# One-hot matrices of a PEER expert mixer moved from GpSimd to VectorE, and adaLN columns fetched for two channel groups at once

## The chip, the cores and the metric

The kernel runs on one core of a Trainium2 chip. The metric is the device time of one execution in microseconds (us); less is better. The engines are TensorE (PE, with its weight loads PEld), VectorE (DVE), ScalarE (ACT), GpSimd (POOL) and SyncE (SP, which here only issues DMA transfers). Each engine runs its own instructions strictly in order and waits at an instruction until the semaphores that it needs have been raised.

## The reference

One decoder layer on a sequence of 1024 rows of 1024 channels. Cut to what matters here:

```python
mod = jnp.einsum('bd,de->be', silu_c, w_ada[l]) + b_ada[l]
shift1, scale1, gate1, shift2, scale2, gate2 = jnp.split(mod, 6, axis=-1)
h = modulate(rms_norm(x, norm1_w[l]), shift1, scale1)   # h * (1 + scale) + shift
proj = jnp.einsum('btd,de->bte', h, w_in[l])
...                                                     # GLA, gMLP, output projection
h2 = modulate(rms_norm(x, norm2_w[l]), shift2, scale2)
y2 = peer(h2, ...)     # for each row: 8 heads x 16 of 16384 experts
x = x + gate2[:, None, :] * y2

# in peer, for a block of 128 rows, ii its 128 expert numbers a row, gg their weights
u = expert_down[ii]
a = jax.nn.gelu(jnp.einsum('pd,ped->pe', xx, u), approximate=False)
vv = expert_up[ii]
return jnp.einsum('pe,ped->pd', gg * a, vv)
```

## The kernel before

**Start.** `x_first` loads the transposed input (8 tiles xt of 128x512, line L975), squares it and makes a row of reciprocal norms, `rrow`. `ada_cols(k)` makes the shift and scale columns (`mod`, `scol`) of channel group k (128 channels): it fetches 1 MB of w_ada in four transfers of 128x4x128 (`wada`, L902, runs of 512 bytes) and weights and sums its eight 128-row pieces into two accumulators `adc`, one for each half of w_ada's rows. The first piece of a half goes through ScalarE (L907), the other three through VectorE (L913, 128x256 each). TensorE then sums the accumulators over partitions (L918), and VectorE makes `mod` and `scol` (L919, L920). `h_first(k)` calls `ada_cols(k + 1)`, multiplies xt by `rrow` on GpSimd (L1004), and `h_split` makes the two halves hTh (ScalarE, L991) and hTl (VectorE, L996) of h, on which the matmuls of the first projection (mm, L173 to L175) wait. The weights of the projection, `wt`, come by the same queue of SyncE as `wada` (L1034) and are split into wh (ScalarE, L1037) and wl (GpSimd or VectorE, L1039).

**Middle.** From some 70 to 1390 us the dense projections, GLA, gMLP, routing, and from about 840 us the first blocks of the expert mixer, beside each other.

**Last stretch.** From 1390 us the remaining expert work runs alone, with its own pools (`own` is true). `peer_stream` walks a list of entries. A gather (GpSimd issues it, L442) brings for each of 128 lanes one row of 8 KB, an expert's u and v, into one of the buffers `uv`; VectorE forms the dot products with h (L496 twice an entry, or L452 once for a direct entry); ScalarE makes gelu and weight `r` and a weighted one-hot matrix `W` (L498 to L508; `rd`, `Wd` for a direct entry); TensorE adds W times v to `acc` (L515), which frees the buffer. Three small matrices steer this. `E` (L593, 128x256, from `ea` that ScalarE makes at L592 into its only buffer) selects which row of the block each lane serves. `e` (the tile `e2` of `entry_list`, L485, 128x128, one an entry, made 8 entries ahead) is the one-hot matrix that `W` is scaled from; its buffer is free once the `W` of nine entries before has been made. `Wr` (L533) is the same for rare rows. With `own`, all three are made on GpSimd, which also issues the gathers. The index of a gather comes from `ts_` (ScalarE, L467, two buffers) by `jk` (VectorE, L470 and L482).

Which engine makes what is written in the code; in what order an engine's instructions stand comes from a scheduler that simulates a timeline, so it can shift when a cost changes.

## Time and profile before

| quantity | value |
|---|---|
| median of 3 runs | 1671.41 us (1666.29 to 1672.44) |
| the profiled execution | 1661.6 us, span 1659.9 us |
| mean granted clock of TensorE | 0.936 |
| busy: PE, DVE, POOL, ACT | 1438.1, 1070.9, 887.5, 778.0 us |

The busy times are averages over stages: at the start (0 to 45 us) and in the holes of the last stretch TensorE is far from busy, and a change there is read from these windows, not from the share over the span. In a table of windows the busy columns stand in the order PE, PEld, DVE, ACT, POOL; a DMA share of about 1.0 means that all 16 DMA engines were moving data all the time.

### The profile page before, as it was taken

What the parts mean: (1) busy time and instruction counts of PE and PEld (TensorE: products, weight loads), DVE (VectorE), ACT (ScalarE), POOL (GpSimd) and SP (SyncE); (2) the same over time, 40 slices, a digit from 0 to 9 for tenths busy, and PEclk for the clock granted to TensorE, in tenths of its full rate; (3) what the DMA queues carried; (4) which work ended last, traced back from release to release, by engine and by line L of the source; (5) the groups of instructions that cost most, each with busy time, mean ns of one, the idle gap of its engine ahead of it and who ended that gap; (6) DMA issues with size and microseconds to landing.
All of it is one profiled execution on the core that took longest, in us unless ns stands there. A gap on an engine that the chain in (4) does not pass through costs nothing. (4 is left out here: it accounts for less than half of the span.)

```text
span 1659.9 us, 20529 instructions
## 1 busy us (share of the span) xinstructions
PE 1438.1 (87%) x6113; PEld 1078.2 (65%) x6113; DVE 1070.9 (65%) x2862; ACT 778.0 (47%) x1716; POOL 887.5 (53%) x761
## 2 busy tenths in 40 slices
PE   4999889999998998788889999989789954798894
PEld 2768757888768886567667777767578832353452
DVE  6773654111456469977987778788885476576653
ACT  4453323332446355735446665555455344444442
POOL 4232237543375338756666877556575425655750
PEclk7999989999999999999999999989899975899998
DMA  9643533223377338746756788768756364897992
GB/s 272 235 175 98 173 121 106 93 91 133 101 241 256 119 115 295 251 153 230 260 188 204 282 319 295 281 213 300 275 213 230 114 232 155 346 415 274 410 412 89
DMA packets 132635, 363.83 MB, mean 219 GB/s; under 512 B 17577, under 2 KB 36265, under 8 KB 116386
## 3 DMA queue, kind: packets, MB, share of 16 engines
q0 software_dynamic: 30816, 178.14, 28.5%
q1 hardware_dynamic: 78464, 132.15, 24.2%
q10 hardware_dynamic: 23234, 52.14, 8.8%
q8 instruction: 49, 0.80, 0.2%
q14 instruction: 72, 0.59, 0.1%
HBM read 336.44 MB, written 25.94 MB: 218 GB/s over the span
## 5 line engine op out<-in xcount | busy, mean ns | idle before, releaser
L1039 POOL TENSOR_TENSOR wl<-wt,wh 128x512 fp32r<-128x512 f32 x257 | 364.3, 1424 | 386.5 <-ACT wh L1037 328.1
L174 PE MATMUL mm<-wl,hTh 128*128 128x512 f32 x896 | 366.3, 409 | 10.3 <-DVE wl L1039 5.6
L1037 ACT ACTIVATE wh<-wt 128x512 fp32r<-128x512 f32 x368 | 228.4, 627 | 308.1 <-PE mm L175 184.8
L175 PE MATMUL mm<-wh,hTl 128*128 128x512 f32 x896 | 357.4, 404 | 3.0 <-DVE hTl L996 3.0
L173 PE MATMUL mm<-wh,hTh 128*128 128x512 f32 x896 | 339.5, 413 | 20.2 <-DVE sg L1240 6.4
L173 PEld LDWEIGHTS mm<-wh,hTh 128*128 128x128 f32 x896 | 172.8, 194 | 71.8 <-DVE sg L1240 7.7
L174 PEld LDWEIGHTS mm<-wl,hTh 128*128 128x128 f32 x896 | 173.2, 193 | 59.2 <-POOL wl L1039 9.2
L1039 DVE TENSOR_TENSOR wl<-wt,wh 128x512 fp32r<-128x512 f32 x111 | 100.0, 903 | 158.6 <-ACT wh L1037 146.4
L175 PEld LDWEIGHTS mm<-wh,hTl 128*128 128x128 f32 x896 | 172.6, 193 | 43.3 <-DVE hTl L996 3.1
L173 PE MATMUL mm<-hTh,wh 128*128 128x512 f32 (+1 forms) x448 | 167.2, 375 | 18.7 <-ACT hTh L169 6.4
L175 PE MATMUL mm<-hTh,wl 128*128 128x512 f32 (+1 forms) x448 | 158.2, 371 | 9.7 <-POOL wl L1039 7.2
L174 PE MATMUL mm<-hTl,wh 128*128 128x512 f32 (+1 forms) x448 | 163.9, 366 | 0.0
L442 POOL DMA_INDIRECT uv<-in_tab_dram,ix x94 | 102.7, 1093 | 71.6 <-PE acc L515 24.4
L496 DVE SCALAR_TENSOR_TENSOR uv<-uv,hps 128x512 f32<-128x512 f32 x148 | 97.8, 683 | 54.6 <-PE hps L495 33.3
L524 DVE SCALAR_TENSOR_TENSOR vl<-uv,r,vh 128x512 fp32r<-128x512 f32 x92 | 91.8, 1026 | 34.7 <-ACT vh L523 29.5
L173 PEld LDWEIGHTS mm<-hTh,wh 128*128 128x128 f32 x448 | 86.4, 194 | 35.4 <-ACT hTh L169 7.1
L515 PE MATMUL acc<-uv,W 128*128 128x512 f32 x192 | 98.9, 641 | 4.4 <-ACT W L508 2.9
L175 PEld LDWEIGHTS mm<-hTh,wl 128*128 128x128 f32 x448 | 85.6, 193 | 24.3 <-POOL wl L1039 8.2
L174 PEld LDWEIGHTS mm<-hTl,wh 128*128 128x128 f32 x448 | 86.5, 193 | 13.5 <-DVE hTl L170 0.2
L494 PE MATMUL hps<-hh,E 128*128 128x512 f32 x148 | 77.8, 529 | 17.7 <-DVE uv L496 12.3
L515 PE MATMUL acc<-uv,Wd 128*128 128x512 f32 x128 | 61.3, 628 | 9.1 <-ACT Wd L456 7.2
L186 DVE MAX8 tv<-so 128x8 f32<-128x128 f32 x128 | 28.5, 277 | 62.1 <-ACT so L1397 62.1
(955 smaller groups left out, 2727.9 us busy)
## 6 DMA issues: line engine op xcount, KB each, us to landing
wt<-in_w_inp_dram SPq DMA_DIRECT2D x224, 256.0 KB
wt<-in_w_qp_dram SPq DMA_DIRECT2D x80, 256.0 KB
wada<-in_w_ada_dram SPq DMA_DIRECT2D x32, 512.0 KB
wt<-in_w_outp_dram SPq DMA_DIRECT2D x64, 256.0 KB
wada<-in_w_ada_dram SPq DMA_DIRECT2D x32, 256.0 KB
s_d<-so ACTq DMA_DIRECT2D x32, 256.0 KB
xr<-in_x_dram ACTq DMA_DIRECT2D x8, 512.0 KB
x_d<-x ACTq DMA_DIRECT2D x8, 512.0 KB
```

The costliest lines, as they stand in the source:

```text
L173: nc.tensor.matmul(ps, lh, rh, start=first, stop=False)
L174: nc.tensor.matmul(ps, lh, rl, start=False, stop=False)
L175: return nc.tensor.matmul(ps, ll, rh, start=False, stop=last).ins
L186: nc.vector.max(v, st)
L442: nc.gpsimd.indirect_dma_start(out=uv[:], out_offset=None, in_=tab, in_offset=bass.IndirectOffsetOnAxis(ap=ix, axis=0))
L494: nc.tensor.matmul(hps, Ej, hh[:, sl], start=True, stop=False)
L496: nc.vector.scalar_tensor_tensor(uv[:, sl], uv[:, sl], 1.0, hps, op0=OP.mult, op1=OP.mult, accum_out=r[:, 2 + n:3 + n])
L515: nc.tensor.matmul(acc[:, sl], W, v[:, sl], start=first, stop=last)
L524: nc.vector.scalar_tensor_tensor(vl, v, r[:, 5:6], vh.bitcast(F32), op0=OP.mult, op1=OP.subtract)
L1037: nc.scalar.activation(wh, wt, AF.Identity)
L1039: eng.tensor_tensor(wl, wt, wh.bitcast(F32), op=OP.subtract)
```

## The change

Three edits. `E` is made on VectorE everywhere (the list `EP` goes). `e2` and `Wr` are made on VectorE when `own` is true. `ada_cols(kp)` serves two channel groups: its transfers are 128x2x256 (runs of 1 KB), still 32 transfers of 256 KB in all; an accumulator has 128x512 elements, so that ScalarE has 8 instructions in place of 16, VectorE 24 of 128x512 (L909) in place of 48 of 128x256, and `mod` and `scol` are made 4 times in place of 8. It is called for even k only.

```diff
--- before.py
+++ after.py
@@ -56,7 +56,6 @@
 RP2 = .42
 DA = 8
 FP = 15
-EP = (True,)
 WLM = 2
 WLM2 = 3
 WLM3 = 99
@@ -67,7 +66,6 @@
 VB = 2
 RA2 = 1.3
 RP3 = .5
-AS = 1
 HA = (range(8), ())
 YA = True
 YP = (4,)
@@ -482,7 +480,7 @@
         nc.vector.scalar_tensor_tensor(jk, ts_[:, 0:n], slot1[:, 0:1], ts_[:, 2 * n:3 * n],
                                        op0=OP.is_equal, op1=OP.mult, accum_out=r[:, 1:2])
         e2 = pq.tile([P, P], F32 if own else F32R, name="e2", bufs=pl["ahead"] + 2)
-        nc.gpsimd.tensor_scalar(e2, iota[:, int(lane0(b)):int(lane0(b)) + P], ts_[:, 3 * n:3 * n + 1], None, op0=OP.is_equal)
+        (nc.vector if own else nc.gpsimd).tensor_scalar(e2, iota[:, int(lane0(b)):int(lane0(b)) + P], ts_[:, 3 * n:3 * n + 1], None, op0=OP.is_equal)
         return pl, Ej, blk, r, uv, hr, e2
 
     def entry_dot(ent):
@@ -530,7 +528,7 @@
         y = ul.tile([P, 2 * D], F32, name="yr", tag="uv")
         nc.scalar.dma_start(y[:, :D], yr_d[gi])
         W = pl["pq"].tile([P, P], F32, name="Wr", tag="e2", bufs=pl["ahead"] + 2)
-        nc.gpsimd.tensor_scalar(W, iota[:, :P], rcol[gi][:, bi:bi + 1], None, op0=OP.is_equal)
+        (nc.vector if pl["own"] else nc.gpsimd).tensor_scalar(W, iota[:, :P], rcol[gi][:, bi:bi + 1], None, op0=OP.is_equal)
         return W, y
 
     def rare_keep(pl, gi, acc):
@@ -590,7 +588,7 @@
         ea = pl["pq"].tile([P, eb * P], F32, name="ea", bufs=1)
         E = pl["pq"].tile([P, eb * P], F32R, name="E", bufs=pl["ebufs"])
         nc.scalar.activation(ea[:, :n], iota[:, :n], AF.Abs, bias=mid[:, j:j + 1])
-        (nc.gpsimd if pl["own"] in EP else nc.vector).tensor_scalar(E[:, :n], ea[:, :n], hw[:, 1:2], None, op0=OP.is_le)
+        nc.vector.tensor_scalar(E[:, :n], ea[:, :n], hw[:, 1:2], None, op0=OP.is_le)
         return E
 
     def await_routing(b, done=routed):
@@ -893,31 +891,32 @@
                     nc.vector.scalar_tensor_tensor(acc, wt, sc[:, k:k + 1], acc, op0=OP.mult, op1=OP.add)
                 yield acc
 
-        def ada_cols(k):
+        def ada_cols(kp):
             accs = []
+            w2 = 2 * P
             for hf_ in range(2):
-                wa = t4("wada").rearrange("p (a c f) -> p a c f", a=4, c=2)
-                src = w_ada[hf_ * 512:(hf_ + 1) * 512, :].rearrange("(a p) n -> p a n", p=P)
-                for c in range(2):
-                    nc.sync.dma_start(wa[:, :, c], src[:, :, c * D + k * P:c * D + (k + 1) * P])
-                acc = gl.tile([P, 2, P], F32, name="adc", bufs=4)
+                acc = gl.tile([P, 2, w2], F32, name="adc", bufs=3)
                 for a in range(4):
-                    w_, s_ = wa[:, a], sc[:, 4 * hf_ + a:4 * hf_ + a + 1]
-                    if a < AS:
-                        nc.scalar.activation(acc if a == 0 else w_, w_, AF.Identity, scale=s_)
-                        if a:
-                            nc.gpsimd.tensor_tensor(acc, acc, w_, op=OP.add)
-                    elif a == 0:
-                        nc.vector.tensor_scalar(acc, w_, s_, None, op0=OP.mult)
+                    q = 4 * hf_ + a
+                    if a % 2 == 0:
+                        wa = t4("wada").rearrange("p (a c f) -> p a c f", a=2, c=2)
+                        src = w_ada[q * P:(q + 2) * P, :].rearrange("(a p) n -> p a n", p=P)
+                        for c in range(2):
+                            nc.sync.dma_start(wa[:, :, c], src[:, :, c * D + kp * w2:c * D + (kp + 1) * w2])
+                    if a == 0:
+                        nc.scalar.activation(acc, wa[:, 0], AF.Identity, scale=sc[:, q:q + 1])
                     else:
-                        nc.vector.scalar_tensor_tensor(acc, w_, s_, acc, op0=OP.mult, op1=OP.add)
+                        nc.vector.scalar_tensor_tensor(acc, wa[:, a % 2], sc[:, q:q + 1], acc, op0=OP.mult, op1=OP.add)
                 accs.append(acc)
-            ps = auxt([P, 2])
+            ps = auxt([P, 2, 2])
             for c in range(2):
-                for i, acc in enumerate(accs):
-                    nc.tensor.matmul(ps[:, c:c + 1], acc[:, c], ones[:, 0:1], start=i == 0, stop=i == 1)
-            nc.vector.tensor_tensor(mod[:, k:16:KD], ps, badat[:, k:16:KD], op=OP.add)
-            nc.vector.scalar_tensor_tensor(scol[:, k:k + 1], mod[:, KD + k:KD + k + 1], 1.0, n1t[:, k:k + 1],
+                for j in range(2):
+                    for i, acc in enumerate(accs):
+                        nc.tensor.matmul(ps[:, c, j:j + 1], acc[:, c, j * P:(j + 1) * P], ones[:, 0:1], start=i == 0, stop=i == 1)
+            ks = slice(2 * kp, 2 * kp + 2)
+            nc.vector.tensor_tensor(mod.rearrange("p (c k) -> p c k", c=2)[:, :, ks], ps,
+                                    badat.rearrange("p (c k) -> p c k", c=2)[:, :, ks], op=OP.add)
+            nc.vector.scalar_tensor_tensor(scol[:, ks], mod[:, KD + 2 * kp:KD + 2 * kp + 2], 1.0, n1t[:, ks],
                                            op0=OP.add, op1=OP.mult)
 
         def ada_row(c, r):
@@ -999,8 +998,8 @@
         ada_cols(0)
 
         def h_first(k):
-            if k + 1 < KD:
-                ada_cols(k + 1)
+            if k % 2 == 0 and k + 2 < KD:
+                ada_cols(k // 2 + 1)
             nc.gpsimd.tensor_tensor(xts[k], xts[k], rrow, op=OP.mult)
             h_split(k)
```

The lines of the changed kernel are numbered 2 lower up to L895 and 1 lower behind it. Where the scheduler puts the instructions, at three places:

VectorE at the start, before, from `dg` (a step of `rrow`) to the second hTl (`adc` are the accumulators, each row one or several instructions, xN their count):

```order
L944 TENSOR_TENSOR dg<-ident,rstd 128x512
L919 TENSOR_TENSOR mod<-aux,badat 128x2
L913 SCALAR_TENSOR_TENSOR adc<-wada,sc,adc 128x256
L920 SCALAR_TENSOR_TENSOR scol<-mod,n1t 128x1
L913 SCALAR_TENSOR_TENSOR adc<-wada,sc,adc 128x256 x4
L919 TENSOR_TENSOR mod<-aux,badat 128x2
L913 SCALAR_TENSOR_TENSOR adc<-wada,sc,adc 128x256
L920 SCALAR_TENSOR_TENSOR scol<-mod,n1t 128x1
L913 SCALAR_TENSOR_TENSOR adc<-wada,sc,adc 128x256 x4
L996 TENSOR_TENSOR hTl<-xt,hTh 128x512
L913 SCALAR_TENSOR_TENSOR adc<-wada,sc,adc 128x256 x2
L996 TENSOR_TENSOR hTl<-xt,hTh 128x512
```

VectorE at the same place, changed:

```order
L943 TENSOR_TENSOR dg<-ident,rstd 128x512
L909 SCALAR_TENSOR_TENSOR adc<-wada,sc,adc 128x512 x2
L1038 TENSOR_TENSOR wl<-wt,wh 128x512
L917 TENSOR_TENSOR mod<-aux,badat 128x2x2
L919 SCALAR_TENSOR_TENSOR scol<-mod,n1t 128x2
L909 SCALAR_TENSOR_TENSOR adc<-wada,sc,adc 128x512 x5
L995 TENSOR_TENSOR hTl<-xt,hTh 128x512 x2
L909 SCALAR_TENSOR_TENSOR adc<-wada,sc,adc 128x512
L917 TENSOR_TENSOR mod<-aux,badat 128x2x2
L919 SCALAR_TENSOR_TENSOR scol<-mod,n1t 128x2
```

Between the first `scol` and the first hTl nine instructions of 128x256, one `mod` and one `scol` stood; now five of 128x512 stand there, and the next `scol` comes for two groups at once.

GpSimd in the last stretch, before, some 1413 to 1440 us of the trace:

```order
L442 DMA uv<-in_tab_dram,dix_147 128x2048
L485 TENSOR_SCALAR e_12855<-iota,ts__12845 128x128
L593 TENSOR_SCALAR E<-ea,hw 128x256
L485 TENSOR_SCALAR e_12903<-iota,ts__12893 128x128
L485 TENSOR_SCALAR e_12925<-iota,ts__12915 128x128
L593 TENSOR_SCALAR E<-ea,hw 128x256
L485 TENSOR_SCALAR e_12959<-iota,ts__12949 128x128
L485 TENSOR_SCALAR e_12988<-iota,ts__12978 128x128
L593 TENSOR_SCALAR E<-ea,hw 128x256
L485 TENSOR_SCALAR e_13026<-iota,ts__13016 128x128
L275 TENSOR_TENSOR tl<-tsel,th 128x112
L442 DMA uv<-in_tab_dram,ix 128x2048 x2
L442 DMA uv<-in_tab_dram,dix_147 128x2048
L442 DMA uv<-in_tab_dram,ix 128x2048 x6
```

GpSimd at the same place, changed (`tl` is a step of the routing):

```order
L440 DMA uv<-in_tab_dram,dix_147 128x2048
L273 TENSOR_TENSOR tl<-tsel,th 128x112
L440 DMA uv<-in_tab_dram,dix_147 128x2048 x2
L273 TENSOR_TENSOR tl<-tsel,th 128x112
L440 DMA uv<-in_tab_dram,ix 128x2048 x2
L440 DMA uv<-in_tab_dram,dix_147 128x2048
L440 DMA uv<-in_tab_dram,ix 128x2048 x11
```

The six `e` and three `E` that stood between two gathers have left; two `tl` are all that stands among the gathers now.

VectorE in the last stretch, before, some 1507 to 1530 us of the trace:

```order
L432 TENSOR_TENSOR hl<-h2l,hh 128x1024
L165 TENSOR_SCALAR fs<-fs 128x1
L496 SCALAR_TENSOR_TENSOR uv,r<-uv,hps 128x512 x2
L573 SCALAR_TENSOR_TENSOR fin<-fin,fs,fw 128x1024
L452 SCALAR_TENSOR_TENSOR uv,rd<-uv,h2l 128x1024 x2
L564 TENSOR_TENSOR fin<-acc,g2row 128x1024
L452 SCALAR_TENSOR_TENSOR uv,rd<-uv,h2l 128x1024 x5
L565 TENSOR_TENSOR fin<-fin 128x1024
L470 SCALAR_TENSOR_TENSOR jk,r<-ts__13709,slot_65 128x16
L470 SCALAR_TENSOR_TENSOR jk,r<-ts__13731,slot_65 128x16
```

VectorE at the same place, changed:

```order
L591 TENSOR_SCALAR E<-ea,hw 128x256
L571 SCALAR_TENSOR_TENSOR fin<-fin,fs,fw 128x1024
L494 SCALAR_TENSOR_TENSOR uv,r<-uv,hps 128x512 x2
L591 TENSOR_SCALAR E<-ea,hw 128x256
L430 TENSOR_TENSOR hl<-h2l,hh 128x1024
L591 TENSOR_SCALAR E<-ea,hw 128x256 x3
L450 SCALAR_TENSOR_TENSOR uv,rd<-uv,h2l 128x1024 x2
L562 TENSOR_TENSOR fin<-acc,g2row 128x1024
L450 SCALAR_TENSOR_TENSOR uv,rd<-uv,h2l 128x1024 x5
L468 SCALAR_TENSOR_TENSOR jk,r<-ts__13657,slot_65 128x16
L483 TENSOR_SCALAR e_13667<-iota,ts__13657 128x128
```

The dots of the direct entries (L450) now stand behind five `E` and in front of `e`.

## Rows read from the trace of the kernel before

**Rows 1.** The page: span; busy us, share and instructions of each engine.

```profile
span 1659.9 us, 20529 instructions
...
PE 1438.1 (87%) x6113; PEld 1078.2 (65%) x6113; DVE 1070.9 (65%) x2862; ACT 778.0 (47%) x1716; POOL 887.5 (53%) x761
```

**Rows 2.** Windows at the start: window, length, busy by engine, clock, DMA share, GB/s.

```profile
30.00:35.00 5.00, 4.21 (x9) 2.62 (x9) 5.00 (x4) 2.43 (x5) 5.00 (x5) 0.50 1.14 310
35.00:40.00 5.00, 2.00 (x8) 1.86 (x8) 5.00 (x7) 2.06 (x4) 4.02 (x3) 0.50 0.86 257
40.00:45.00 5.00, 3.85 (x9) 3.09 (x10) 4.97 (x12) 2.02 (x5) 2.06 (x1) 0.50 0.31 92
45.00:50.00 5.00, 5.00 (x25) 3.98 (x25) 3.76 (x9) 3.02 (x6) 1.32 (x1) 0.84 1.01 296
...
70.00:75.00 5.00, 5.00 (x24) 3.70 (x22) 0.94 (x1) 2.90 (x6) 1.39 (x6) 1.00 1.02 417
```

**Rows 3.** VectorE's timeline at the start: start, length, operation, idle before.

```profile
22.27 0.87 DVE L913 SCALAR_TENSOR_TENSOR adc<-wada,sc,adc 128x256 f32<-128x256 f32 x2
...
29.43 5.84 DVE L913 SCALAR_TENSOR_TENSOR adc<-wada,sc,adc 128x256 f32<-128x256 f32 x4
...
36.59 1.22 DVE L920 SCALAR_TENSOR_TENSOR scol<-mod,n1t 128x1 f32<-128x1 f32 x1
...
40.42 0.68 DVE L996 TENSOR_TENSOR hTl<-xt,hTh 128x512 fp32r<-128x512 f32 x1
```

**Rows 4.** Timeline of GpSimd at the start.

```profile
26.81 10.99 POOL L1004 TENSOR_TENSOR xt<-xt,rrow 128x512 f32<-128x512 f32 x8 [0.79 <-ACT rrow L949]
```

**Rows 5.** Timeline of TensorE at the start.

```profile
41.15 2.08 PE L175 MATMUL mm<-wh,hTl 128*128 128x512 f32 x4 [2.98 <-DVE hTl L996]
```

**Rows 6.** Windows of the last stretch, columns as in group 2.

```profile
1380.00:1400.00 20.00, 6.00 (x20) 4.92 (x20) 14.80 (x115) 8.66 (x23) 9.31 (x13) 0.50 0.24 66
...
1420.00:1440.00 20.00, 14.33 (x37) 7.92 (x36) 12.09 (x42) 9.43 (x35) 11.97 (x10) 0.77 0.71 270
1440.00:1500.00 60.00, 57.78 (x178) 31.20 (x177) 40.23 (x186) 26.85 (x85) 33.38 (x39) 1.00 1.01 413
1500.00:1520.00 20.00, 15.21 (x33) 6.57 (x32) 11.02 (x31) 9.78 (x26) 13.94 (x14) 0.83 0.89 328
1520.00:1540.00 20.00, 16.69 (x50) 8.02 (x48) 14.21 (x38) 8.01 (x33) 9.74 (x11) 1.00 0.59 208
```

**Rows 7.** Groups by line, 1390 to 1615 us: count, busy, mean ns, idle.

```profile
L496 DVE SCALAR_TENSOR_TENSOR uv<-uv,hps 128x512 f32<-128x512 f32 x82 | 54.1, 684 | 27.9 <-PE hps L495 14.3 <-DMA uv<-in_tab_dram,ix 13.1 <-issue 0.2
...
L593 POOL TENSOR_SCALAR E<-ea,hw 128x256 fp32r<-128x256 f32 x24 | 26.7, 1114 | 4.2 <-ACT ea L592 3.8 <-PE hps L495 0.2
...
L592 ACT ACTIVATE ea<-iota,mid 128x256 f32<-128x256 f32 x24 | 12.1, 505 | 20.6 <-POOL E L593 18.9 <-DVE hw L581 1.5
```

**Rows 8.** Line L593 over the span: least, median and largest ns.

```profile
L593 DVE TENSOR_SCALAR E<-ea,hw x46: 229/286/2402, 844.0 to 1239.5; 128x128 fp32r<-128x128 f32 x46
```

**Rows 9.** Timeline of GpSimd, 1405 to 1435 us.

```profile
1416.34 1.02 POOL L442 DMA_INDIRECT uv<-in_tab_dram,dix  x1 [0.17 <-issue]
...
1418.90 0.60 POOL L485 TENSOR_SCALAR e<-iota,ts__12893 128x128 f32<-128x128 f32 x1
...
1430.47 1.70 POOL L485 TENSOR_SCALAR e<-iota,ts__13016 128x128 f32<-128x128 f32 x1 [3.81 <-ACT W L508]
...
1433.86 1.35 POOL L442 DMA_INDIRECT uv<-in_tab_dram,ix  x1 [1.30 <-PE acc L515]
```

**Rows 10.** Timeline of VectorE, 1405 to 1435 us.

```profile
1427.71 0.28 DVE L470 SCALAR_TENSOR_TENSOR jk<-ts__13016,slot 128x56 f32<-128x56 f32 x1 [2.50 <-ACT ts__13016 L467]
```

**Rows 11.** Timeline of ScalarE, 1499 to 1532 us.

```profile
1510.58 0.51 ACT L592 ACTIVATE ea<-iota,mid 128x256 f32<-128x256 f32 x1 [2.33 <-POOL E L593]
...
1518.24 0.51 ACT L592 ACTIVATE ea<-iota,mid 128x256 f32<-128x256 f32 x1 [1.97 <-POOL E L593]
1518.65 0.19 ACT L453 ACTIVATE rd<-rd 128x1 f32<-128x1 f32 x1
```

## The prediction

> **What bounds the kernel now.** I read the page first. TensorE is busy 87% of the span, VectorE 65%, GpSimd 53% [rows 1]: over most of the run TensorE sets the pace, and an edit elsewhere pays only where TensorE stands still. So I looked with windows for such stretches near the lines that the change touches. There are two.
>
> At the start TensorE is busy 4.21, 2.00 and 3.85 us of the three windows of 5 us from 30 to 45 us, so 4.94 us are idle, and its granted clock is 0.50, the lower of its two levels (1.2 GHz); the six windows from 45 to 75 us read 5.00 of 5 [rows 2]. In two of these three windows VectorE is busy 5.00 of 5 us, in the third 4.97: it is the bound there. Its timeline shows with what: between its two pieces of work for the first hTl it must pass the sums for the next channel groups, and the first hTl runs at 40.42 us only [rows 3]. TensorE's timeline has the matmul that needs it at 41.15 us, after 2.98 us of waiting for exactly that [rows 5].
>
> In the last stretch the 16 DMA engines are the bound most of the time: their share is 1.01 from 1440 to 1500 us, with 413 GB/s [rows 6]. Where it falls, time is lost: 0.71 from 1420 to 1440 us, 0.89 and 0.59 in the two windows behind 1500 us. Against 1.01 that is 20 x 0.30 = 6.0, 20 x 0.12 = 2.4 and 20 x 0.42 = 8.4 us of transfer time, 16.8 us in two holes. A third one lies ahead of the first gather (0.24 from 1380 to 1400 us). In all three GpSimd makes E and e between, or ahead of, the gathers.
>
> **The start, costed.** Before, VectorE makes nine sums of 128x256 (and small steps) between 29.43 and 40.42 us. Four of them took 5.84 us, 1.46 each [rows 3], while two took 0.87 us, 0.43 each, before GpSimd began its eight multiplications by rrow (26.81 to 37.80 us, 1.37 each) [rows 4]. A scol of one column took 1.22 us in the same time. So beside GpSimd the price is per instruction, more than per column. Now five sums of 128x512 stand there. The lower bound of one is 1.46 us (price per instruction): 5 x 1.46 = 7.3, the first hTl at 29.5 + 7.3 = 36.8, a gain of 3.6 us. The upper bound is 2.92 (price per column): 2.8 of them until 37.8 us, then 2.2 x 0.87 = 1.9, the first hTl at 39.7, a gain of 0.7 us. Because of the scol I take a value near the lower bound: **3 us**. From then on TensorE has the second group's hTh at once, since its scol came with the first, and goes on without a gap, as it did before from 45 us; so the 3 us reach the end of this projection. I give nothing for TensorE's clock coming back earlier: it rose in the window 45 to 50 us (0.84), after TensorE had worked on from 41.15 us, and would rise as much behind the new restart. Nor do I give anything for the fetch itself. Longer runs move more (417 GB/s from 70 to 75 us, where whole rows of 2 and 4 KB are fetched, against 310 GB/s here) [rows 2], but VectorE, not the transfers, is full at this time. ScalarE's 8 instructions saved lie beside its waits for scol.
>
> **The last stretch, costed.** What leaves GpSimd: 24 E of 1114 ns, 26.7 us [rows 7], and 52 e and Wr of about 0.60 us [rows 9], 31 us. What VectorE gets: the nearest row is its own E of 128x128 in the middle of the run, 229 ns at least, 286 at the median [rows 8]. 52 x 0.286 = 14.9 us, and 24 E of twice the columns at between 0.29 and 0.57 us, I take 0.4, 9.6 us: 24.5 us in 225. VectorE is busy 40.23 of the 60 us from 1440 to 1500 [rows 6]; a share of 24.5 x 60/225 = 6.5 makes 46.7, 78%. So I cost this at nothing, covered by the transfers; if that cover went, it would be up to 24.5 us.
>
> Hole at 1430 us: the gather at 1416.34 is followed by the next one at 1433.86 [rows 9]. Between them GpSimd makes six e and three E; ScalarE, whose only `ea` buffer is freed by E, stands behind them, hence VectorE waits 2.50 us for the `ts_` that ScalarE gives late [rows 10], its dots come late, then W (GpSimd's next e waits 3.81 us for it), then the matmul that frees a buffer for the gather. With E at 0.4 us, VectorE's 2.50 us go at least; at most the 6.0 us of transfers come back. In between, nearer to the first: **3.5 us**.
>
> Hole behind 1500 us: ScalarE and GpSimd go in lock-step, ea, E, ea, E; ScalarE waits 2.33 us ahead of one ea, 1.97 ahead of another [rows 11], in all 18.9 us over the stretch [rows 7]. The weight `rd` of direct entries stands behind the last ea and comes at 1518.65 us, and with it the matmuls that free buffers. On VectorE E costs some 0.5 us less and is not stretched by a neighbour. Five such steps save 2.5 us at least; at most the two windows' 10.8 us. But now the direct entries' dots stand behind the E, so that part of the gain is lost: **3 us**. Hole ahead of 1400 us: three E and two e left out ahead of the first gather, of which VectorE does the same in between its own work: **1 us**.
>
> What is late next: in the rest of the stretch the transfers (1.01) and, towards the end, TensorE, which keep their work; a shift of the gathers is carried to the end.
>
> **Sum.** 3 + 3.5 + 3 + 1 = 10.5 us. The profiled execution took 1661.6 us, so 1651.1 for its like; it was 9.8 us below the median of 1671.41, and from this I predict 1671.4 - 10.5 = **1661 us**.
>
> **A rule against it.** VectorE's E took up to 2402 ns where the median is 286 [rows 8], so these instructions can be held up. By the Trainium skill, "SBUF — State Buffer", section "Who interferes with whom", a tensor_scalar in a two-port mode takes the port pair that VectorE and GpSimd share, for its whole length, and the other engine blocks fully, gathers' descriptors included. That they are held up agrees with the row; that it happens beside gathers no row shows. By that rule the 76 moved instructions and the 72 gathers would hold each other up: an estimate from the median, 76 x 0.29 = 22 us at most, would turn the sum into 1671.4 - 10.5 + 22 = 1683 us; the trace alone gives the sum above. Its chance is part of the first rival's, where VectorE loses the same time by another wait.
>
> **Rivals.**
> Slower: VectorE becomes the bound in the last stretch. Its `e` waits in order for the W of nine entries before, and W follows that entry's second dot by about 1 us of ScalarE's work; what is queued behind it, the next dots, waits too. An entry costs VectorE two dots of 684 ns [rows 7], two jk of 0.28 [rows 10], one e of 0.29 and half an E, 0.2: 2.4 us, against 2.4 to 2.5 us in which its 1 MB comes at 413 GB/s. It decides as soon as waits for W or for a gather's issue on GpSimd exceed 0.1 us an entry. At 0.5 us on 40 entries the price is 20 us less the 10.5 gained: 1681 us. For it speaks the close balance; against it, that VectorE stood idle 27.9 us ahead of these dots, waiting for hps and data [rows 7], so that small waits hide. 16 in 100.
>
> Given back: the holes are set by buffers that matmuls free, not by GpSimd (the gather at 1433.86 waited 1.30 us for acc, after GpSimd had already waited 3.81 us) [rows 9]. Then GpSimd waits longer at the gather, and only the start and 1 or 2 us remain: 1667 us. 25 in 100.
>
> The start doesn't pay: sixteen fetches (4 MB) stand ahead of the first wt on SyncE's queue where eight (2 MB) stood. At 310 GB/s 2 MB are 6.8 us; if the first matmul, so far at 30.5 us, comes 3 us later, the start's gain is gone: 1664 us. For it speaks the full DMA share there, against it that TensorE waits until some 40 us anyway. 9 in 100.
>
> **Numbers.** The likeliest, 50 in 100, is 1661 us, by the bounds of its terms (0.7 to 3.6, 2.5 to 6.0, 2.5 to 10.8 less what the new order costs, 0 to 1.2) between 1654 and 1666. Faster or slower by 0.5%, 8.4 us, is about what a measurement of this kernel can tell from no change: below 1663 or above 1680. Faster: four fifths of the likeliest, a third of the third rival, a quarter of the second, 0.50. Slower: two thirds of the first rival, 0.11, and a little for places in the middle where the scheduler put the interleaved instructions otherwise, 0.13 in all. No change that can be told: 0.37. The range from 1648 to 1676 leaves the worse half of the first rival above and gains beyond all bounds below.
>
> **What would show it.** Right: at the start the first hTl near 37.5 us and no idle time of TensorE between 38 and 65 us; in the last stretch no gap of over 8 us between gathers near 1430 us, ScalarE's waits for E (18.9 us) below 8 us, DMA shares of 0.85 and more in the windows of the holes, VectorE busy some 24 us more there. Wrong: VectorE's e waiting for W by more than 0.3 us an entry, E or e on VectorE at a median above 0.6 us, gathers longer than before, or the same holes with GpSimd idle and waiting for acc.

## The result and the profile after

The changed kernel took 1653.26 us at the median of 10 runs (1650.64 to 1657.56), the kernel before 1669.83 us in the runs beside it: ratio 0.9914, 95% interval 0.9896 to 0.9931, by which it is about 14 us less (the two medians lie 16.6 us apart). In a later session, beside new runs of the kernel before on one chip, the ratio was 0.9934 (0.9916 to 0.9952), 11 us less. The prediction said 10.5 us less.

The page of the kernel after, where [rows 1] stood before:

```profile
span 1648.5 us, 20446 instructions
...
PE 1440.4 (87%) x6113; PEld 1077.6 (65%) x6113; DVE 1069.7 (65%) x2906; ACT 775.4 (47%) x1708; POOL 816.3 (50%) x685
```

GpSimd's busy time is down from 887.5 us (53%) to 816.3. VectorE's is nearly unchanged in sum, but not by stage: it is 6.9 us less up to the 1301st matmul of the projections (199.8 to 192.9), 6.9 us less in the middle, and 10.9 us more in the last stretch (164.2 to 175.1, from 50 us behind the last matmul of the projections on).

Windows at the start (columns as in [rows 2]):

```profile
30.00:35.00 5.00, 3.85 (x9) 2.36 (x9) 4.96 (x4) 3.60 (x6) 5.00 (x3) 0.64 1.08 359
35.00:40.00 5.00, 2.93 (x16) 2.68 (x17) 5.00 (x4) 0.72 (x1) 5.00 (x4) 0.70 1.01 343
40.00:45.00 5.00, 5.00 (x17) 3.11 (x16) 4.90 (x7) 1.45 (x3) 3.44 (x3) 0.62 0.44 138
45.00:50.00 5.00, 5.00 (x31) 4.32 (x30) 4.94 (x10) 3.35 (x6) 0.00 (x0) 1.00 0.09 32
```

TensorE is idle 1.15 and 2.07 us in the first two windows and no longer from 40 to 45 us: 3.22 us in place of 4.94. VectorE is still full there. Its timeline, and the matmul on TensorE that waits for the first hTl, beside [rows 3] and [rows 5]:

```profile
28.70 8.57 DVE L909 SCALAR_TENSOR_TENSOR adc<-wada,sc,adc 128x512 f32<-128x512 f32 x5
37.19 3.43 DVE L995 TENSOR_TENSOR hTl<-xt,hTh 128x512 fp32r<-128x512 f32 x2
```

```profile
39.00 2.08 PE L173 MATMUL mm<-wh,hTl 128*128 128x512 f32 x4 [1.42 <-DVE hTl L995]
```

The five sums of 128x512 took 8.57 us, 1.71 each, and the first hTl came at 37.19 us in place of 40.42. It took about 1.7 us itself, where it took 0.68 before, so its matmul came at 39.00 in place of 41.15: of 3.2 us, 2.2 reach TensorE here.

The last stretch, windows as in [rows 6], then groups as in [rows 7] and a row of VectorE's waits (us in total, times, longest):

```profile
1380.00:1400.00 20.00, 8.43 (x26) 6.53 (x26) 14.62 (x121) 8.19 (x29) 7.20 (x9) 0.50 0.49 165
...
1420.00:1440.00 20.00, 17.38 (x46) 8.19 (x46) 8.67 (x28) 7.29 (x24) 8.76 (x9) 1.00 0.80 303
...
1480.00:1500.00 20.00, 19.77 (x60) 10.36 (x58) 18.47 (x91) 12.87 (x33) 5.98 (x8) 1.00 0.83 322
1500.00:1520.00 20.00, 15.03 (x41) 6.87 (x40) 14.29 (x29) 8.91 (x28) 5.94 (x4) 1.00 0.93 364
1520.00:1540.00 20.00, 15.52 (x42) 8.28 (x43) 13.84 (x63) 9.05 (x39) 11.75 (x11) 0.89 0.86 320
```

```profile
L590 ACT ACTIVATE ea<-iota,mid 128x256 f32<-128x256 f32 x24 | 12.1, 505 | 6.1 <-DVE E L591 3.0 <-DMA thl<-ts_d 2.0 <-DVE pos L296 1.1
...
L591 DVE TENSOR_SCALAR E<-ea,hw 128x256 fp32r<-128x256 f32 x24 | 8.6, 357 | 5.6 <-ACT ea L590 4.6 <-issue 0.7 <-PE hps L493 0.2
```

```profile
DVE e L483 <- ACT W L506: 5.4, 8, 1.3
```

E takes 357 ns on VectorE, ScalarE waits 3.0 us for it in place of 18.9, and e waits 5.4 us for W, 0.11 us an entry. The share of the transfers is higher in all four windows that had a hole before (0.24, 0.71, 0.89, 0.59), but there is a new hole, 0.83 from 1480 to 1500 us. (The windows stand at fixed times, and the changed kernel is 3.4 us ahead when the last stretch begins.)

**A measure by stages.** Runs of one kernel lie up to 19 us apart (e7_runs1k, 1647.57 to 1666.75), so single profiles are compared by stage. Three marks are read from each timeline: the start of the 1301st matmul of the projections, the start of the last one, and the end of VectorE's last step on `fin`. In the kernel after these are

```profile
423.79 0.39 PE L173 MATMUL mm<-wh,hTl 128*128 128x512 f32 x1
```

```profile
1328.86 0.39 PE L173 MATMUL mm<-hTh,wl 128*128 128x512 f32 x1
```

```profile
1633.45 1.28 DVE L571 SCALAR_TENSOR_TENSOR fin<-fin,fs,fw 128x1024 f32<-128x1024 f32 x1 [0.73 <-POOL fs L164]
```

so the stages are 423.79 us, then 1328.86 - 423.79 = 905.07 us, then 1633.45 + 1.28 - 1328.86 = 305.87 us. Read in the same way for all runs with a profile:

| kernel | to 1301st matmul | middle | last stretch |
|---|---|---|---|
| before | 430.14 | 902.12 | 313.19 |
| changed | 423.79 | 905.07 | 305.87 |
| changed, again (e11_after) | 424.23 | 909.05 | 306.08 |
| start alone (e1_start) | 424.92 | 913.19 | 314.76 |
| E, e, Wr on VectorE alone (e2_last) | 428.36 | 905.58 | 305.71 |
| E alone (e3_E) | 429.07 | 911.12 | 302.94 |
| e, Wr alone (e4_onehots) | 428.77 | 907.75 | 311.15 |
| two ea buffers (e8_ea2) | 429.85 | 907.33 | 312.77 |
| E moved, GpSimd given other work (e12_dummy) | 430.72 | 907.85 | 316.87 |
| start and E (e9_start_E) | 422.80 | 906.22 | 300.91 |
| the same, two ea buffers (e10_start_E_ea2) | 422.93 | 909.12 | 308.42 |
| start, 64 fetches, runs of 512 B (e5_runs512) | 424.44 | 905.58 | 316.20 |
| start, 64 fetches, runs of 1 KB (e7_runs1k) | 425.39 | 905.71 | 304.33 |
| start, sums of 256 columns (e6_narrow) | 426.56 | 897.87 | 312.71 |

In before, e2, e3, e4, e8 and e12 the instructions stand in the same order on every engine until the last stretch. Their first stage lies within 428.4 and 430.7 us (mean 429.5), their middle between 902.1 and 911.1 us (mean 907.0). So the middle differs by 9 us between executions of one and the same program, and the first profile of the kernel before had the shortest middle of the six. The changed kernel, its second run, e1, e9 and e10 also share their order until the last stretch: first stage 422.8 to 424.9 us (mean 423.7), middle 905.1 to 913.2 us (mean 908.5). The start therefore gained 5.8 us; of the middle no difference can be told. The last stretch stands in another order in nearly every kernel, and each kernel but the changed one was profiled once, so a difference of a few us there is not only the work's but also the order's.

### The profile page after: what moved, and what is told of

Read it like the earlier page. It is cut to its first block, busy times and chain, and to the rows that moved or that the text cites. A ratio compares the mean times of both kernels' runs of the same rounds, so it can differ in the third digit from the quotient of the medians.

```text
span 1648.5 us, 20446 instructions
## 1 busy us (share of the span) xinstructions
PE 1440.4 (87%) x6113; PEld 1077.6 (65%) x6113; DVE 1069.7 (65%) x2906; ACT 775.4 (47%) x1708; POOL 816.3 (50%) x685
## 5 line engine op out<-in xcount | busy, mean ns | idle before, releaser
L1038 POOL TENSOR_TENSOR wl<-wt,wh 128x512 fp32r<-128x512 f32 x257 | 360.6, 1409 | 368.5 <-ACT wh L1036 344.4
L1036 ACT ACTIVATE wh<-wt 128x512 fp32r<-128x512 f32 x368 | 228.0, 627 | 314.0 <-PE mm L173 177.3
L171 PE MATMUL mm<-hTh,wh 128*128 128x512 f32 (+1 forms) x448 | 168.5, 378 | 10.9 <-ACT hTh L167 4.6
L522 DVE SCALAR_TENSOR_TENSOR vl<-uv,r,vh 128x512 fp32r<-128x512 f32 x92 | 81.6, 915 | 36.4 <-ACT vh L521 33.7
L492 PE MATMUL hps<-hh,E 128*128 128x512 f32 x148 | 76.3, 519 | 22.3 <-DVE uv L494 10.9
L521 ACT ACTIVATE vh<-uv,r 128x512 fp32r<-128x512 f32 x92 | 62.2, 714 | 3.8 <-PE acc L523 1.4
```

Source lines behind the costliest of these rows:

```text
L171: nc.tensor.matmul(ps, lh, rh, start=first, stop=False)
L492: nc.tensor.matmul(hps, Ej, hh[:, sl], start=True, stop=False)
L521: nc.scalar.activation(vh, v, AF.Identity, scale=r[:, 5:6])
L522: nc.vector.scalar_tensor_tensor(vl, v, r[:, 5:6], vh.bitcast(F32), op0=OP.mult, op1=OP.subtract)
L1036: nc.scalar.activation(wh, wt, AF.Identity)
L1038: eng.tensor_tensor(wl, wt, wh.bitcast(F32), op=OP.subtract)
```

## The experiments

**e1_start: the start alone.** E, e and Wr go back to GpSimd in the changed kernel (of the three, the edits of e and E, with arguments left out as ...):

```diff
-        (nc.vector if own else nc.gpsimd).tensor_scalar(e2, ...)
+        nc.gpsimd.tensor_scalar(e2, ...)
-        nc.vector.tensor_scalar(E[:, :n], ...)
+        (nc.gpsimd if pl["own"] else nc.vector).tensor_scalar(E[:, :n], ...)
```

> The changed kernel with E, e and Wr of the last stretch back on GpSimd, so that only the columns for two groups are left of the change. Theory A (both parts pay and add): the projection's matmuls run about 6.3 us ahead of the kernel before from 130 to 800 us, and the time is 6 us less, ratio 0.996. Rival B (all of the gain comes from the start, the last stretch gave nothing that the middle did not take back): ratio 0.991, 14 us less. Rival C (the middle takes the start's lead back, since it is bound by other things): lead of 6 us until 800 us, none at 1330 us, ratio 1.000.

Measured: 1663.24 us against 1667.69, ratio 0.9977 (0.9959 to 0.9996). The first stage is 424.92 us, 4.6 us less than the mean of the kernel before; the last stretch, 314.76 us, has gained nothing. By the time, the start alone is worth 4 us (0.7 to 6.8): a part of the gain, not the whole of it. Rival B is out. Rival C, that the middle takes the lead back, is only narrowly excluded by the time. The profiled execution, the slowest of the twelve, had lost its lead at the last matmul of the projections (1338.10 us), but over the five kernels with the new start and the six with the old one this matmul lies at 1332.3 and 1336.4 us at the mean, with a spread of 3 to 4 us.

**e2_last: the last stretch alone.** The moves of E, e and Wr in the kernel before.

> The kernel before with E, e and Wr of the last stretch on VectorE, so that only the moved matrices are left of the change. Theory A: 8 us less, ratio 0.995, with ScalarE's waits for E near 3 us in place of 18.9 and the holes of the transfers near 1430 and 1520 us smaller. Rival B: ratio 1.000. Rival C: nearly the whole gain, ratio 0.992.

Measured: 1656.71 us, ratio 0.9946 (0.9919 to 0.9973), 9 us less; last stretch 305.71 us, as in the changed kernel. With e1: 0.9977 x 0.9946 = 0.992, between the two measurements of the whole. Both parts pay, and they add.

**e3_E and e4_onehots: E alone, e and Wr alone.** In the kernel before, one of

```diff
-        (nc.gpsimd if pl["own"] in EP else nc.vector).tensor_scalar(E[:, :n], ...)
+        nc.vector.tensor_scalar(E[:, :n], ...)
```

```diff
-        nc.gpsimd.tensor_scalar(e2, ...)
+        (nc.vector if own else nc.gpsimd).tensor_scalar(e2, ...)
```

> The kernel before with only the 24 matrices E of the last stretch on VectorE; e and Wr stay on GpSimd. Theory A (the lock-step of ScalarE and GpSimd over the single ea buffer makes the holes): the larger part of the last stretch's gain, 5 to 6 us, ratio 0.9965, ScalarE's waits for E near 3 us. Rival D (the 52 small matrices between the gathers make the holes by delaying GpSimd): under 2 us, ratio 0.999, the holes as before.

> The kernel before with only e and Wr on VectorE; E stays on GpSimd. Theory A: 2 us less, ratio 0.999, ScalarE's waits for E still over 12 us. Rival D: 6 us less, ratio 0.996, with gathers one behind the other near 1430 us.

Measured: E alone 1657.21 us, ratio 0.9939 (0.9914 to 0.9963), last stretch 302.94 us, the whole gain and some more. e and Wr alone 1666.54 us, ratio 0.9992 (0.9970 to 1.0014), last stretch 311.15 us: 2 us by the stage, and by the interval of the time at most 5. E on GpSimd, groups of e4:

```profile
L593 POOL TENSOR_SCALAR E<-ea,hw 128x256 fp32r<-128x256 f32 x24 | 28.8, 1198 | 13.9 <-ACT ea L592 4.4 <-PE tps L464 2.5 <-ACT r L504 2.2
```

Rival D, that the 52 small matrices make the holes, is out: GpSimd loses 35 us of work in e4 (147.0 to 112.1 us, from 50 us behind the last matmul of the projections on) and nearly nothing happens.

**e8_ea2: is it the hand-over of the buffer?** The kernel before with a second ea buffer:

```diff
-        ea = pl["pq"].tile([P, eb * P], F32, name="ea", bufs=1)
+        ea = pl["pq"].tile([P, eb * P], F32, name="ea", bufs=2 if pl["own"] else 1)
```

> The kernel before, all three matrices on GpSimd, with two ea buffers in the last stretch in place of one: ScalarE need not wait for the E before. The length from the start of the last projection matmul to the end of the output's last step is the measure (313.2 us in the kernel before, 302.9 with E alone on VectorE). Theory F (the holes come from the hand-over of the one ea buffer between ScalarE and GpSimd): 303 to 306 us, ratio 0.995. Rival G (they come from the time that E takes on GpSimd, ahead of gathers and of other work that waits for E): 310 us or more, ratio 0.999.

Measured: 1664.93 us, ratio 0.9982 (0.9963 to 1.0001), last stretch 312.77 us. ScalarE waits less for E, 12.3 us in place of 18.9:

```profile
L592 ACT ACTIVATE ea<-iota,mid 128x256 f32<-128x256 f32 x24 | 11.8, 505 | 13.9 <-POOL E L593 12.3 <-DMA thl<-ts_d 1.4
```

but the stretch is as long as before; by the time the gain is 3 us, and its interval reaches from nothing to 6. Theory F, the lock-step over the one buffer, would have had 7 to 10 us less of last stretch, and falls; rival G's sign came.

**e12_dummy: is it E's delay or GpSimd's time?** E alone on VectorE as in e3, and beside each E an operation of the same shape on GpSimd whose result is not used:

```diff
         nc.vector.tensor_scalar(E[:, :n], ea[:, :n], hw[:, 1:2], None, op0=OP.is_le)
+        if pl["own"]:
+            Ed = pl["pq"].tile([P, eb * P], F32, name="Ed", bufs=1)
+            nc.gpsimd.tensor_scalar(Ed[:, :n], iota[:, :n], hw[:, 1:2], None, op0=OP.is_le)
```

> E alone on VectorE (302.9 us of last stretch), and GpSimd given back as much work: for each E one operation of the same shape and kind on GpSimd whose result nobody reads. Theory H (what counts is how soon E itself is there, 0.35 us on VectorE against 0.94 to 3 on GpSimd): 303 to 306 us, ratio 0.995. Rival I (what counts is the time that GpSimd's queue loses ahead of gathers): 310 us or more, ratio 0.999.

Measured: 1663.9 us, ratio 0.9982 (0.9964 to 1.0001), last stretch 316.87 us (the profiled execution was the slowest of the twelve). By the time 3 us are left of e3's 10, with an interval from nothing to 6. So most of e3's gain is gone, by the stage all of it, although E still comes from VectorE: rival I's sign, not theory H's. ScalarE waits for E as little as in e3, 7.0 us against 7.9, so these waits don't make the difference of 14 us. The two rows, e3 first:

```profile
L592 ACT ACTIVATE ea<-iota,mid 128x256 f32<-128x256 f32 x24 | 12.1, 505 | 11.2 <-DVE E L593 7.9 <-DMA thl<-ts_d 1.9 <-POOL tlq L275 1.3
```

```profile
L592 ACT ACTIVATE ea<-iota,mid 128x256 f32<-128x256 f32 x24 | 12.1, 505 | 9.3 <-DVE E L593 7.0 <-DMA thl<-ts_d 1.8
```

GpSimd's timeline in the hole behind 1500 us shows where a part of it went (the two kernels' last projection matmuls start 1.6 us apart). E alone, e3: the first and the last of the seven gathers that stand in this window, and the instruction behind them:

```profile
1499.82 0.94 POOL L442 DMA_INDIRECT uv<-in_tab_dram,dix  x1 [1.93 <-PE acc L515]
...
1516.03 0.95 POOL L442 DMA_INDIRECT uv<-in_tab_dram,dix  x1 [0.30 <-ACT Wd L456]
1526.59 1.62 POOL L485 TENSOR_SCALAR e<-iota,ts__13709 128x128 f32<-128x128 f32 x1 [9.61 <-ACT ts__13731 L467]
```

With the dummies, e12:

```profile
1501.71 0.95 POOL L442 DMA_INDIRECT uv<-in_tab_dram,dix  x1 [1.61 <-DVE smq L204]
...
1511.72 3.36 POOL L596 TENSOR_SCALAR Ed<-iota,hw 128x256 f32<-128x256 f32 x2
...
1516.66 1.96 POOL L596 TENSOR_SCALAR Ed<-iota,hw 128x256 f32<-128x256 f32 x2
...
1520.40 6.04 POOL L596 TENSOR_SCALAR Ed<-iota,hw 128x256 f32<-128x256 f32 x4
1526.62 1.06 POOL L442 DMA_INDIRECT uv<-in_tab_dram,dix  x1 [0.17 <-issue]
```

In e3 seven gathers are issued within 16.2 us; the wait behind them is for ScalarE. In e12 the same block's seven take 24.9 us, because the dummies stand among them, four of them 6.04 us in a row, stretched to 1.5 us each. Counted from the last matmul of the projections, e12's 12th gather, behind the hole at 1430 us, comes 6.1 us later than e3's, its 41st 13.2 and its last 12.8. The reading that fits is that the time in GpSimd's queue ahead of gathers that could go out is what counts. Two things are not separated from it. The dummies also hold up VectorE: an E there takes 0.43 us at the mean with them, 0.37 without. And the scheduler set the order anew in each kernel.

**e5_runs512, e7_runs1k, e6_narrow: what pays at the start?** All three from e1. In e5 and e7 each transfer is cut in two, over the columns (runs of 512 bytes) or over the rows (runs of 1 KB). The slices are given in words:

```diff
-                        for c in range(2):
-                            nc.sync.dma_start(wa[:, :, c], src[:, :, <256 columns>])
+                        for c in range(2):
+                            for j in range(2):
+                                nc.sync.dma_start(wa[:, :, c, j * P:(j + 1) * P], src[:, :, <128 columns of group j>])   # e5
+                                nc.sync.dma_start(wa[:, j, c], src[:, j, <256 columns>])                                # e7
```

In e6 the fetch stays, and each sum is made in two instructions, one a group:

```diff
-                        nc.vector.scalar_tensor_tensor(acc, wa[:, a % 2], sc[:, q:q + 1], acc, ...)
+                        for j in range(2):   # av, wv: the 128 columns of group j
+                            nc.vector.scalar_tensor_tensor(av, wv, sc[:, q:q + 1], av, ...)
```

> The start alone (E, e, Wr on GpSimd), columns for two groups and sums of 128x512, but each transfer cut in two over the columns: 64 transfers of 128 KB with runs of 512 bytes. Against its twin with runs of 1 KB, whose instructions stand in the same order on VectorE. Theory A (VectorE's instruction count sets the start, the fetch is beside it): the lead of the projection's matmuls over the kernel before at 300 us is within 1 us of the twin's. Rival E (the longer runs are what pays): at least 3 us less lead than the twin, and 300 GB/s in place of 350 between 20 and 35 us.

> The twin: the same, but each transfer cut in two over the rows: 64 transfers of 128 KB with runs of 1 KB. Both theories: about the lead of the start alone, 6 us at 300 us; a loss against it would be the price of twice the transfers.

> The start alone, fetched as in the change (runs of 1 KB, two groups), but the sums made in 48 instructions of 128x2x128 on VectorE and 16 on ScalarE, as many as before. Theory A: the first hTl comes as late as in the kernel before, near 40 us or later, and the lead at 60 us (3.3 us in the changed kernel) goes to under 1 us. Rival E: the lead stays within 1 us of the start alone, since the fetch is unchanged.

Measured: e5 1660.07 us, ratio 0.9947 (0.9924 to 0.9969); e7 1654.88 us, 0.9928 (0.9896 to 0.9960); e6 1659.89 us, 0.9939 (0.9920 to 0.9958). These whole times can't be laid to the start: with each new start the scheduler set the middle and the last stretch in another order (e6 has the shortest middle of all, e7 a last stretch of 304.33 us with E on GpSimd). So the first stage is read. e5: 424.44 us, e7: 425.39 us. One window, 25 to 30 us, of e1, e5 and e7 in this order:

```profile
25.00:30.00 5.00, 4.65 (x20) 4.05 (x18) 2.40 (x5) 2.55 (x5) 3.27 (x3) 0.50 1.09 350
```

```profile
25.00:30.00 5.00, 3.37 (x16) 3.28 (x16) 1.99 (x3) 1.82 (x4) 4.55 (x4) 0.50 0.95 286
```

```profile
25.00:30.00 5.00, 3.80 (x19) 3.71 (x17) 1.83 (x4) 1.62 (x3) 4.12 (x4) 0.50 0.94 296
```

The transfers of 128 KB move 286 and 296 GB/s in place of 350, and the run length makes 3% of difference here (also over the five windows from 10 to 35 us). TensorE's first projection matmul comes at 37.36 and 39.02 us in place of 30.67, since wt stands behind the slower fetch. And still the first stage is as short as e1's to within a microsecond. (VectorE's order is the same in e5 and e7 up to some 61 us only.) Rival E, the longer runs, is out, and so is the rival that a late wt costs the start its gain: only three sums stand ahead of the first hTl in e7, which comes at 34.64 us,

```profile
29.53 5.18 DVE L911 SCALAR_TENSOR_TENSOR adc<-wada,sc,adc 128x512 f32<-128x512 f32 x3
34.64 3.42 DVE L997 TENSOR_TENSOR hTl<-xt,hTh 128x512 fp32r<-128x512 f32 x2
```

and TensorE catches up by having no gap later. In e6 nine sums of 128x256 stand there again:

```profile
28.12 11.86 DVE L911 SCALAR_TENSOR_TENSOR adc<-wada,sc,adc 128x256 f32<-128x256 f32 x9
39.90 0.68 DVE L997 TENSOR_TENSOR hTl<-xt,hTh 128x512 fp32r<-128x512 f32 x1
```

They take 1.32 us each, the first hTl is as late as before (39.90 us), the lead at the 61st matmul is gone (-0.2 us, where e1 has 2.1 and the changed kernel 3.3), and the first stage, 426.56 us, keeps half of the gain: the half that the narrower sums don't take away.

**e9_start_E, e10_start_E_ea2, e11_after: a better version?** The changed kernel with e and Wr back on GpSimd (e9), that with two ea buffers (e10), and the changed kernel again, on one chip.

> The changed kernel with e and Wr of the last stretch back on GpSimd: columns for two groups and E alone on VectorE. Theory A: the start's lead of 5 to 6 us and a last stretch of 303 us (305.9 in the changed kernel), together 15 to 17 us less than before, ratio 0.990, a little under the changed kernel. Rival: e on VectorE is needed once the start is earlier: 0.993 or more.

> The kernel of the run before this one with two ea buffers in the last stretch. Theory F: ScalarE waits for E under 2 us, the last stretch 301 to 303 us, ratio 0.989. Rival: no change against one buffer, since E on VectorE comes back in 0.35 us.

> The changed kernel once more, on the same chip as the runs beside it: ratio 0.991, start of the projection 5 to 6 us ahead, a last stretch of 305 to 307 us, and between the two a lead that differs from the first profile's by some us either way, if that part of the time is the run's and not the change's.

Measured: e9 1650.54 us (1646.39 to 1655.54, 6 runs), ratio 0.9912 (0.9890 to 0.9934); e10 1656.65 us, 0.9946 (0.9926 to 0.9966); the changed kernel 1655.52 us (1652.59 to 1656.97, 6 runs), 0.9934 (0.9916 to 0.9952). e9's last stretch is 300.91 us, 5 us shorter than the changed kernel's, and its median is 5.0 us lower. The two kernels' six runs overlap, and so do the intervals of the ratios, so e9 is likely, not surely, the faster. It beats the kernel before by 15 us. e10 was slower than e9, by the last stretch (308.42 us). Its instructions stand in another order there, and 4.7 of the 7.5 us are lost behind 1500 us, from the 37th gather, counted in the last stretch, to the 41st (25.8 us against 21.0). So a new order alone can move this stretch by as much as the change does.

## Why the prediction was right, point by point

**The sum** was near: 10.5 us predicted, 14 and 11 us measured. The time itself, 1653.3 us against 1661, lies inside the range and just below the 1654 to 1666 us that the bounds of the terms gave. In part this was luck: some terms were too small and some too large, and the mechanism of the last stretch was another one. Of the signs named, the first hTl (37.19 us), ScalarE's waits for E (3.0 us) and TensorE's work without a gap (from 39.00 us on) came. A gap between gathers of 13.1 us near 1430 us, a DMA share of 0.80 from 1420 to 1440 us and VectorE's 10.9 us more in place of 24 did not fit.

**The start** was costed at 3 us and gave 5.8. The term that it costed came out as said: the sums beside GpSimd cost 1.71 us each, between the bounds 1.46 and 2.92 and near the lower one, the first hTl came at 37.2 us (37.5 was named), and at the 61st matmul the lead is 3.3 us. That VectorE and not the fetch is the bound was shown by e5, e6 and e7. What the sum left out are mainly two stalls of TensorE behind the first 75 us. Before, from 60 to 135 us, and after, from 55 to 130 us, waits of TensorE (us in total, times, longest):

```profile
PE mm L175 <- DVE wl L1039: 2.4, 1, 2.4
PE mm L174 <- POOL wl L1039: 1.5, 1, 1.5
```

```profile
PE mm L173 <- DVE wl L1038: 0.8, 1, 0.8
```

The wait for a wl on GpSimd is gone, that for a wl on VectorE has shrunk from 2.4 to 0.8 us: 3.1 us together. Between the means of the six and of the five kernels the lead grows by less, from 3.35 us at the 61st matmul to 5.75 at the 1301st. That the earlier start moved these stalls is not so: e6, without a lead at the 61st matmul, has them shrunk too (0.8 us for a wl, 0.5 for a wh), and this is the half of the gain that it keeps. It comes with the new order of the start; by which step was not followed up. I had looked for idle time of TensorE up to 75 us only.

**The last stretch** was costed at 7.5 us and gave 8.1 (mean of before and e1, 314.0, less the mean of the changed kernel's two runs and e2, 305.9). The 52 e and Wr that left GpSimd had been priced at 31 us from one row; they took 36.2. By holes, measured from the last projection matmul: the first gather comes 2.5 us earlier and the fifth 5.0 (1 us was predicted for the first hole, since I counted the three E ahead of the first gather and not those among the next ones); the hole at 1430 us gave nothing (3.5 predicted; the lead is 5.1 us at the 9th gather and 4.9 at the 12th, behind the hole); between the gathers 37 and 41, behind 1500 us, 5.6 us (3 predicted). The lead of the first hole does not last: it is 1.0 us at the 36th gather, 2.7 us being lost in the new hole ahead of the 32nd. So in this kernel it is the hole behind 1500 us that makes most of the gain that is left at the end. In e2, with the same moves, 5.1 us of lead were left at the 36th gather: where the gain is made depends on the order too. That the hole at 1430 us stayed is seen on GpSimd's timeline:

```profile
1400.92 0.94 POOL L440 DMA_INDIRECT uv<-in_tab_dram,dix  x1 [0.30 <-PE tps L463]
...
1409.20 0.95 POOL L440 DMA_INDIRECT uv<-in_tab_dram,dix  x1 [6.89 <-DVE uv L450]
1412.47 0.93 POOL L440 DMA_INDIRECT uv<-in_tab_dram,dix  x1 [2.32 <-PE tps L463]
...
1425.58 1.63 POOL L440 DMA_INDIRECT uv<-in_tab_dram,ix  x1 [8.71 <-PE tps L463]
```

The gather at 1412.47 is followed by the next one at 1425.58, 13.1 us later (17.5 us before), with GpSimd idle for most of it, and the gap ahead of the gather at 1409.20 has grown instead. The profile names tps, but the gather's index, counted in order, had been ready since 1393.81 us, and an acc, which frees a buffer, ended on TensorE at 1425.30 us: it waits for a buffer. Here the rival "given back" was right, and I should have seen it in [rows 9], where GpSimd had waited 3.81 us for W ahead of the same gather.

**The step that failed** is the chain ea, E, ScalarE, VectorE. The prediction said that ScalarE's waits for E delay the rest, and took the gain from them. e8 took a third of these waits away and gained little or nothing; e12 kept the waits as short as e3 and lost most or all of the gain when GpSimd was given its time back. What the runs show in their place is GpSimd's time: an E there, 1.1 us at the mean, stands ahead of gathers whose buffers are free. e7 fits this from the other side: with E on GpSimd, but four E done by 1507.6 us, its last stretch is 304.33 us. Its timeline, first and last E of the four that this window shows, and a gather behind them:

```profile
1499.64 1.37 POOL L591 TENSOR_SCALAR E<-ea,hw 128x256 fp32r<-128x256 f32 x1
...
1506.41 1.17 POOL L591 TENSOR_SCALAR E<-ea,hw 128x256 fp32r<-128x256 f32 x1 [0.64 <-ACT ea L590]
...
1522.75 1.55 POOL L440 DMA_INDIRECT uv<-in_tab_dram,dix  x1 [0.30 <-issue]
```

In e1, whose order is that of the changed kernel until the last stretch, the last E of this block starts at 1522.47 us and one of its gathers stands behind it:

```profile
1508.96 0.93 POOL L591 TENSOR_SCALAR E<-ea,hw 128x256 fp32r<-128x256 f32 x1
...
1522.47 0.92 POOL L591 TENSOR_SCALAR E<-ea,hw 128x256 fp32r<-128x256 f32 x1 [0.63 <-ACT ea L590]
1523.56 1.06 POOL L440 DMA_INDIRECT uv<-in_tab_dram,dix  x1 [0.17 <-issue]
```

How far the order alone goes is seen from the time between the 37th and the 41st gather. With E on VectorE it is 21.0 to 23.0 us in the changed kernel, e2, e3 and e9, but 25.8 in e10. With E on GpSimd it is 27.1 and 26.2 in the kernel before and e1, but 23.4 and 23.5 in e8 and e4, and 20.2 in e7. So E's place on GpSimd makes a long hole likely, and where the scheduler puts each E decides; no run held the order fixed.

Why the 52 e and Wr count for so little on the same queue was argued, not shown: GpSimd waits at them for W at times when its next gather would wait for a buffer anyway.

**The rule of the Trainium skill** ("SBUF — State Buffer", "Who interferes with whom") that a tensor_scalar of VectorE in a two-port mode and GpSimd block each other is not borne out here beside gathers: on VectorE e took 0.268 to 0.418 us, E 0.343 to 0.485, although 22 of the 48 e and 10 of the 24 E ran beside one (whether they run in such a mode no row says), and a gather took 0.94 us at the median against 1.02 before. Beside GpSimd's computing the trace agrees with it. In the middle of the changed kernel an E of 128x128 took 4.48 us, where the median there is 0.285. It ended 0.1 us behind the last of four tensor_tensors that GpSimd ran beside it one behind the other. VectorE first, then GpSimd:

```profile
898.72 4.48 DVE L591 TENSOR_SCALAR E<-ea,hw 128x128 fp32r<-128x128 f32 x1
```

```profile
896.84 3.79 POOL L1241 TENSOR_TENSOR ot<-ot,sg 128x512 f32<-128x512 f32 x3
900.58 1.29 POOL L1038 TENSOR_TENSOR wl<-wt,wh 128x512 fp32r<-128x512 f32 x1
901.83 1.28 POOL L1241 TENSOR_TENSOR ot<-ot,sg 128x512 f32<-128x512 f32 x1
```

So the 2402 ns that the prediction read were such a wait, ending 0.1 us behind a tensor_tensor of GpSimd. In the last stretch only one of the 24 E met computing on GpSimd, since little of it was left there. The rival "VectorE becomes the bound" may have a true part: with E there too, e and Wr on VectorE come with a last stretch that is 3 to 5 us longer (305.7 to 306.1 against 302.9 and 300.9 us), while the E pay 10. By the times e2 and e3 can't be told apart, and what of it is the order's is open.

**The middle** was given no term, and its chance was "a little". No difference can be told, but one execution's middle differs from another's by 9 us, more than either part of the change is worth. That the profiled execution of before lay 9.8 us below the median is for the larger part its short middle, 5.8 us below the mean of the other five.

## What to carry to other kernels

Ask of each piece of work on the engine that issues gathers not how long it is, but whether a gather stands behind it that could go out: moving 24 operations away gained 10 us, moving 52 gained 2. Where a scheduler sets the order anew for each version, single versions can't settle a few us: two that differed by one buffer lay 7.5 us apart. Where an engine is full beside another one's work and pays per instruction, wider instructions can be worth more than a faster fetch, as here. And check a mechanism by putting its cost back in another form: the dummy work told in one run against what the waits in the profile had suggested.

## What the runs showed of the hardware

VectorE's two-input sums beside GpSimd's two-input multiplications cost 1.32 to 1.46 us for 256 columns and 1.71 us for 512, where 512 columns alone took 0.73 to 0.77 us (two in 1.46 and 1.53 us ahead of GpSimd's work in the changed kernel): the price beside GpSimd is nearly one of instructions. The trace shows how. From 30 to 36 us the two engines take turns, one instruction each: a sum ends some 0.28 us (256 columns) or 0.55 us (512) behind the end of a multiplication, and the next multiplication ends 1.12 to 1.16 us behind the sum. GpSimd pays as well: its eight multiplications, 10.99 us before [rows 4], took 12.58.

```profile
25.81 12.58 POOL L1003 TENSOR_TENSOR xt<-xt,rrow 128x512 f32<-128x512 f32 x8 [3.57 <-ACT rrow L948]
```

In the last stretch, too, GpSimd's operation of 128x256, 0.94 us at the median, was stretched to 2.99 us, beside two dots of VectorE with two inputs, 1.21 us each. Transfers of 128 KB moved 286 to 296 GB/s where those of 256 KB with the same runs of 1 KB moved 350, whereas runs of 512 bytes against 1 KB, at 128 KB a transfer, made 3%. At 256 KB a transfer the run length did count: in the same window the kernel before, with runs of 512 bytes, moved 305.
